# The short branch's output product as seven half-block products in two duals, later modulations moved, gates through half-width buffers

## The chip, the cores and the metric

The kernel runs on one core of a Trainium2 chip. The metric is the device time of one execution in microseconds (us); a figure for a kernel is the median of its runs. A profile is one further execution, recorded by the hardware profiler. Engines are named as the profile names them: PE (TensorE: matrix products), DVE (VectorE), ACT (ScalarE), POOL (GpSimd), SP (SyncE, here only a queue that issues transfers).

## The reference, cut to what matters

One layer of a streaming encoder on x of 1024 tokens by 1024 channels, in fp32:

```
h    = rms_norm(x) * (1 + sc1) + sh1                 # sh, sc, g: "modulations", silu(c) @ w_ada + b_ada
proj = h @ w_in                                      # 7168 columns: b, c, v, u, u's gate, gates a and b
y_a  = (b * dwconv3(c * v)) @ w_short_out            # short branch: its operand is called q below
y_b  = silu(layer_norm(dwconv31(u * sigmoid(gl)))) @ w_conf_out
x    = x + g1 * ((sigmoid(ga) * y_a + sigmoid(gb) * y_b) @ w_o)
x    = x + g2 * ffn(rms_norm(x) * (1 + sc2) + sh2)   # SwiGLU, then a last rms_norm
```

## The kernel before, in words

**Numbers.** Each fp32 operand of a product is split in two (`split` L311, `split_w` L198): a high part, cast to fp32r by ACT (L314 for activations, L205 for weights, called `..h` and `wh`), and a low part, source minus high part (`..l` on DVE, L315; `wl`, L206, on DVE or on POOL). `mm3` then needs three matmuls per product of two 128-blocks and 512 tokens: L283 (wh, high), L284 (wh, low), L286 (wl, high). In the changed kernel these are L288, L289, L291; the splits stand at L206, L207, L319 and L320.

**Stages.** Tokens lie on the free axis in two halves h of 512; a channel block is 128 wide. In order on PE: a lead with the first columns of `w_in` and the block `gb`; twelve **duals** (`win_dual`, L565 on) for the other 48 column blocks; the short branch's product `ya` (L757 to L762); the conformer branch's `yb`; `mix` with `w_o`; the feed-forward part. A dual computes four column blocks for both halves by Strassen-Winograd: seven products of half the depth, named "1" "2" "6" "5" "7" "3" "4" in their order, each 2 banks x 4 depth blocks x 3 = 24 matmuls, 168 where the plain form takes 192. Banks x, y, z are three pairs of PSUM banks; a product's result is carried from one bank to the next by ACT copies ("1" into y; "6" and "5" into small tiles `v`, L626) and joined by DVE (L583, L594). The weight blocks of a dual are loaded by SP, added by POOL (L228, L229, L230, L232) and split with the low part on POOL.

**The short branch before.** The q tiles (128 x 1024, eight of them) are finished in the duals, stored to DRAM by SP (L528), and read again during the last dual, number 11: `q_load` (L552) reads two tiles behind each of its products "1", "2", "6", "5" and splits both halves at once. `ya` then runs eight column blocks, each 8 depth blocks x 2 halves x 3 = 48 matmuls, 384 in all, one weight block of `w_short_out` for each column block. Its results are multiplied by the gate a on DVE (L762); the gates were stored to DRAM by the duals, one 128 x 1024 tile at a time (L642, on ACT's queue), and come back by POOL's queue (L760).

**Beside it.** The convolution of 31 taps runs on DVE through all duals (L671, its accumulator in PSUM). Its result u is summed over the blocks on POOL into `tot` (L691, two adds for each block), and `ln_mean` (L698) turns these sums into the mean with two small products `mu`; `ln_square` (L711 to L719) reads u back from DRAM (`cv`) and sums the squares; `ln_rstd` makes `var`. In the kernel before, `mu` follows the first column block of `ya`. The second 24 of the 48 modulations (L264 on DVE: a row product of a loaded 512 KB block with `cs`, sum on the fly) are in `ya` (six behind column blocks, two at the end) and in `yb` (16).

**Order.** Every engine works its own list in order; the lists come from the order of the code through a scheduler. Tiles are taken from rotating pools: `uc` (128 x 1024 tiles: u, q, cv, sc), `g` (128 x 512 tiles: gates, v, sq), `hl` (split halves). A tile can be filled only when the last reader of what lay there before is done, so a load can wait for an engine.

Of the kernel before, what the change touches and what calls it, by code (L numbers as in the profile page):

```python
# [39 lines left out]
P = 128  # L40
# [43 lines left out]
CONV_DUALS = 11.2  # L84
AT_READS = {"7": 4.5, "3": 5.5, "4": 6.5}
# [22 lines left out]
def block_kernel(ctx: ExitStack, tc: tile.TileContext, x0, xT, c, vecs, ada, w_first, w_plain, w_duals,  # L108
# [102 lines left out]
    def dual_units(mats, n, early=False, eng=nc.vector):  # L211
# [7 lines left out]
        def unit(m):  # L219
            if early:  # L220
                get(*{"1": ("11",), "2": ("12",), "6": ("21", "22", "11"), "3": ("12",), "4": ("22",)}.get(m, ()))
            elif m == "1":
                get("11", "12", "21", "22")
            if m in "12":
                return split_w(a["1" + m], n, (), eng)
# [7 lines left out]
            return split_w(a[{"6": "11", "5": "s1", "7": "21", "3": "12", "4": "22"}[m]], n, (), eng)  # L233
# [9 lines left out]
    plan += [(w_short[k], 1024, (), nc.gpsimd) for k in range(KC)]  # L243
# [307 lines left out]
    qT = [[None, None] for _ in range(KC)]  # L551

    def q_load(j):

        t = uc_tile("q", T)
        nc.sync.dma_start(t, q_dram[j])
        for h in range(2):
            qT[j][h] = split(t[:, halves[h]], hl_tile, f"q{j}{h}")

    def win_dual(d, pairs, x, y, z):  # L560
# [4 lines left out]
        def c11(p, e, kind, j, *more):  # L565
# [6 lines left out]
            elif kind == "p":  # L572
                e["t"] = uc_tile(f"p{j}", T + SK - 1)
                nc.vector.memset(e["t"][:, : SK - 1], 0.0)
                e["b"] = [e["t"][:, SK - 1 + h * H : SK - 1 + (h + 1) * H] for h in range(2)]
            else:
                e["t"] = [uc_tile("sig", T) for _ in range(2)]
                e["b"], e["c"] = ([t[:, s] for s in halves] for t in e["t"])
            nc.scalar.activation(e["b"][0], y[p], AF.Sigmoid if kind == "g" else AF.Copy)

        def c22(p, e, kind, j, *more):
# [4 lines left out]
            if kind == "p":  # L586
                e["z"] = src
            else:
                e["z"] = e["c"][1] if kind == "g" else src
                nc.scalar.activation(e["z"], src, AF.Sigmoid, scale=-1.0)  # L590
            return add

        def c12(p, e, kind, j, *more):
# [7 lines left out]
            nc.scalar.activation(e["b"][1], z[p], AF.Sigmoid)  # L601
            return add

        def c21(p, e, kind, j, *more):
# [7 lines left out]
            nc.scalar.activation(e["c"][0], x[p], AF.Sigmoid, scale=-1.0)  # L612

        banks = {"1": x, "6": x, "7": x, "4": x, "2": y, "5": z, "3": z}
        for m in PRODUCTS:
# [15 lines left out]
            if d == len(PAIRS) // 2 - 1 and m in "1265":  # L631
                for j in range(2):
                    q_load(2 * "1265".index(m) + j)
        for e, (kind, j, *more) in zip(st, pairs):
            if kind == "p":
                short_conv(j, e["t"], x)
            elif kind == "q":
                for i in range(2):
                    q_store(j + i)
            elif kind == "g":  # L640
                for g, t in zip((j, *more), e["t"]):
                    nc.scalar.dma_start(gate_dram[g], t)  # L642
# [55 lines left out]
    def ln_mean():  # L698
        mu = []
        for h in range(2):  # L700
            mps = ps_tile("mu")
# [19 lines left out]
    def ln_rstd(sqs):  # L721
        rs = []
        for h in range(2):
            var = ps_tile("var")
# [11 lines left out]
    def act_b(k, h):  # L736
        z = cv[k][:, halves[h]]
        with ExitStack() as order:
            if (KC - 1, 1) in ma:
# [5 lines left out]
    def next_b(k, h):  # L745
# [3 lines left out]
        modulation(24 + KC * h + k)  # L749
# [7 lines left out]
    for j in range(KC):  # L757
        for h, ps in enumerate(col_block(next_w(), qT, (0, 1), "ya")):
            ga = g_tile("ga")
            nc.gpsimd.dma_start(ga, gate_dram["a", j][:, halves[h]])  # L760
            ma[j, h] = s_tile(f"ma{j}{h}")
            ma["ins"] = nc.vector.tensor_tensor(ma[j, h], ps, ga, ALU.mult).ins  # L762
        if j == 0:
# [6 lines left out]
        if j == KC - 2:  # L770
            act_b(0, 0)
        if j < KC - 2:
            modulation(16 + j)


    modulation(22)
    modulation(23)
# [426 lines left out]
```

## Time and profile before

| | us |
|---|---|
| median of 3 runs | 1505.06 |
| lowest and highest run | 1504.25 to 1505.3 |
| span of the profiled execution | 1501.2 |
| time of the profiled execution | 1502.96 |
| of the span: PE busy | 1469.3 |
| DVE busy | 1141.0 |
| ACT busy | 623.1 |
| POOL busy | 538.2 |

The profiled execution took 1.76 us more than its span and lies 2.1 us under the median. Starts in the trace are us from the start of the span. A row of the timeline gives start, duration, engine, line, operation, output<-input and how many instructions are drawn together, then in brackets how long the engine was idle before and what released it. A row of the windows gives for a stretch its length and each engine's busy time with the instructions in brackets, the granted clock of TensorE as a share, the busy share of the DMA engines and GB/s. A row of the waits gives who waited for whom: total, times, longest.

### The profile page before, as it was taken

How to read it: one execution, taken by the hardware profiler on the slowest of the kernel's cores; microseconds unless marked ns; L12 is line 12 of the kernel's file. 1: busy time of each engine (PE TensorE's matmuls, PEld its weight loads, DVE VectorE, ACT ScalarE, POOL GpSimd, SP SyncE). 2: the span in 40 equal slices, each digit the busy share in tenths (PEclk: the TensorE clock that was granted, in tenths of full speed). 3: DMA queues.
4: the chain of work that ended last, by engine and by line, in shares of the span. 5: the costliest groups of instructions: out<-in, count | busy, mean ns of one | idle time of the engine just before them, and what ended most of it. 6: DMA issues, size and time to landing. Idle time of an engine off the chain costs nothing.

```text
span 1501.2 us, 17711 instructions
## 1 busy us (share of the span) xinstructions
PE 1469.3 (98%) x6455; PEld 1202.0 (80%) x6455; DVE 1141.0 (76%) x1569; ACT 623.1 (42%) x896; POOL 538.2 (36%) x467
## 2 busy tenths in 40 slices
PE   6999999999999999999999989999999999999997
PEld 2788888888888788887788868888888888888887
DVE  7994999887887984777767789776666665667755
ACT  4653433443343353244345454444444443222235
POOL 0037777777767773410121001111000016444005
PEclk9999999999999999999999989999999999999999
DMA  9522223232222268555765337544444449998403
GB/s 352 207 64 74 94 71 112 70 108 75 98 71 85 99 261 299 167 175 175 231 207 183 126 98 236 200 169 153 152 149 150 153 148 351 364 324 256 141 28 112
DMA packets 82697, 247.24 MB, mean 165 GB/s; under 512 B 9521, under 2 KB 11697, under 8 KB 82610
## 3 DMA queue, kind: packets, MB, share of 16 engines
q1 hardware_dynamic: 41776, 137.91, 27.4%
q0 software_dynamic: 36944, 95.44, 19.2%
q10 hardware_dynamic: 3890, 12.78, 2.2%
q8 instruction: 50, 0.82, 0.2%
q14 instruction: 37, 0.30, 0.1%
HBM read 183.69 MB, written 62.39 MB: 164 GB/s over the span
## 4 chain that ended last, share of the span: by engine, by line
PE 93%; DVE 4%; issue 1%; ACT 1%; DMA 1%; POOL 0%; POOLq 0%; ACTq 0%; DVEq 0%
PE x L286 11%; PE x L284 11%; PE x L283 10%; PE z L283 7%; PE z L284 7%; PE z L286 7%; PE y L284 6%; PE y L283 6%; PE y L286 6%; PE ya L284 2%; PE mix L286 2%; PE mix L284 2%; PE ya L283 2%; PE ya L286 2%; PE mix L283 2%; PE yb L283 2%
## 5 line engine op out<-in xcount | busy, mean ns | idle before, releaser
L205 ACT CAST wh<-raw 128x1024 fp32r<-128x1024 f32 (+2 forms) x257 | 259.4, 1010 | 482.8 <-PE z L284 122.0
L206 POOL TENSOR_TENSOR wl<-raw,wh 128x1024 fp32r<-128x1024 f32 x92 | 227.2, 2471 | 131.1 <-ACT wh L205 130.9
L206 DVE TENSOR_TENSOR wl<-raw,wh 128x1024 fp32r<-128x1024 f32 (+2 forms) x165 | 188.4, 1142 | 52.7 <-ACT wh L205 50.0
L671 DVE SCALAR_TENSOR_TENSOR c<-diff,vec,c 128x512 f32<-128x512 f32 x248 | 178.6, 751 | 3.3
L930 POOL DMA_DIRECT2D hid<-stage x71 | 37.9, 534 | 358.7 <-DVE stage L323 353.0
L283 PE MATMUL x<-th,wh 128*128 128x512 f32 x240 | 93.4, 389 | 0.0
L284 PE MATMUL x<-tl,wh 128*128 128x512 f32 x240 | 93.4, 389 | 0.0
L286 PE MATMUL x<-th,wl 128*128 128x512 f32 x240 | 93.4, 389 | 0.0
L671 DVE SCALAR_TENSOR_TENSOR c<-u,wsum,c 128x512 f32<-128x512 f32 x112 | 84.1, 751 | 1.8
L264 DVE CUSTOM_DVE_ANT_0 raw<-raw,cs,vec 128x1024 f32<-128x1024 f32 x24 | 35.5, 1486 | 50.6 <-DMA raw<-in_ada 50.6
L283 PE MATMUL z<-th,wh 128*128 128x512 f32 x168 | 65.4, 389 | 0.0
L284 PE MATMUL z<-tl,wh 128*128 128x512 f32 x168 | 65.4, 389 | 0.0
L286 PE MATMUL z<-th,wl 128*128 128x512 f32 x168 | 65.4, 389 | 0.0
L228 POOL TENSOR_TENSOR raw<-raw 128x1024 f32<-128x1024 f32 x12 | 29.8, 2482 | 95.0 <-DVE wl L206 94.2
L322 ACT CAST stage<-g 128x512 fp32r<-128x512 f32 x62 | 38.3, 621 | 52.0 <-DMA hid<-stage 25.1
L323 DVE TENSOR_TENSOR stage<-g,stage 128x512 fp32r<-128x512 f32 x62 | 42.5, 688 | 20.5 <-ACT stage L322 20.4
L956 POOL DMA_DIRECT2D th<-hid x71 | 38.1, 537 | 52.0 <-PE x L286 28.3
L283 PE MATMUL yb<-zsh,wh 128*128 128x512 f32 x128 | 50.0, 391 | 2.8 <-DVE gb L793 2.8
L283 PE MATMUL x<-t2h,wh 128*128 128x512 f32 x120 | 47.7, 400 | 5.1 <-ACT wh L205 2.8
L286 PEld LDWEIGHTS x<-th,wl 128*128 128x128 f32 x240 | 45.1, 188 | 9.4
L283 PEld LDWEIGHTS x<-th,wh 128*128 128x128 f32 x240 | 45.1, 188 | 9.3
L284 PEld LDWEIGHTS x<-tl,wh 128*128 128x128 f32 x240 | 45.1, 188 | 9.3
(1012 smaller groups left out, 4263.8 us busy)
## 6 DMA issues: line engine op xcount, KB each, us to landing
hid<-stage POOLq DMA_DIRECT2D x71, 512.0 KB, 4.0
raw<-in_w_fi SPq DMA_DIRECT2D x50, 512.0 KB, 4.3
raw<-in_w_duals SPq DMA_DIRECT2D x48, 512.0 KB, 3.5
th<-hid POOLq DMA_DIRECT2D x71, 256.0 KB, 5.9
tl<-hid POOLq DMA_DIRECT2D x71, 256.0 KB, 6.0
ada<-in_ada SPq DMA_DIRECT2D x24, 512.0 KB, 5.8
raw<-in_ada SPq DMA_DIRECT2D x24, 512.0 KB, 4.5
raw<-in_w_fo SPq DMA_DIRECT2D x24, 384.0 KB, 6.2
```

What stands on the lines that cost most here:

```text
L205: nc.scalar.copy(wh, raw)
L206: lo = lo_engine.tensor_tensor(wl, raw, f32(wh), ALU.subtract)
L228: eng.tensor_tensor(a["s1"], a["21"], a["22"], ALU.add)
L264: nc.vector.tensor_tensor_reduce(out=raw, in0=raw, in1=cs, scale=1.0, scalar=col(V_ADA, b), op0=ALU.mult, op1=ALU.add, accum_out=modc(b),)
L283: nc.tensor.matmul(ps, wh, xh, start=first, stop=False, skip_group_check=again)
L284: nc.tensor.matmul(ps, wh, xl, start=False, stop=False, skip_group_check=again)
L286: mm3.ins = nc.tensor.matmul(ps, wl, xh, start=False, stop=last, skip_group_check=again).ins
L322: nc.scalar.copy(hi, src)
L323: nc.vector.tensor_tensor(lo, src, f32(hi), ALU.subtract)
L671: tap.ins = nc.vector.scalar_tensor_tensor(out=out, in0=src[:, s : s + H], scalar=wt, in1=acc, op0=ALU.mult, op1=ALU.add).ins
L930: nc.gpsimd.dma_start(hid_dram[key], s)
L956: nc.gpsimd.dma_start(t, hid_dram[key][:, s])
```

## The change

**The product.** `ya` becomes two duals of seven products, in this order of (dual, product): (0,"1") (0,"2") (1,"1") (1,"2"), then "6" "5" "7" "3" "4" of dual 0, then of dual 1. That makes 14 x 24 = 336 matmuls. The weights are cut in half blocks, four for each dual; POOL adds them (eight adds), and splits the low parts of "1" and "2", while DVE splits those of the other five. Half of the q blocks stay in their tiles (`sc[4]` to `sc[7]`), the other four are stored and read again, all four behind product "1" of dual 11. `q_operands` forms and splits the operands product by product (28 splits in place of 16, and 16 sums or differences on DVE). The results are carried from bank to bank as in the other duals.

**Where things stand.** `mu` now comes behind the third product in the code. Nine of the 24 later modulations move into duals 0 to 8 (behind their product "2"), eight into the first half of `yb`, seven into the first half of `mix`. Gates leave the duals as 28 half tiles of 128 x 512 in place of 14 whole tiles, each with a store of its own on ACT's queue; the gates a are read back by SP in place of POOL.

```diff
+MOD_DUALS = 9
...
-    plan += [(w_short[k], 1024, (), nc.gpsimd) for k in range(KC)]
+    ya_order = [(d, m) for d in range(2) for m in "12"] + [(d, m) for d in range(2) for m in PRODUCTS[2:]]
+    ya_units = [dual_units([w_short[d, m] for m in range(4)], 1024, True, nc.gpsimd, {m: nc.vector for m in "65734"})
+                for d in range(2)]
+    plan += [ya_units[d][m] for d, m in ya_order]
...
+    def gate_out(g, h, src, t, scale=1.0):
+
+        nc.scalar.activation(t, src, AF.Sigmoid, scale=scale)
+        nc.scalar.dma_start(gate_dram[g][:, halves[h]], t)
...
     def q_load(j):
 
-        t = uc_tile("q", T)
-        nc.sync.dma_start(t, q_dram[j])
-        for h in range(2):
-            qT[j][h] = split(t[:, halves[h]], hl_tile, f"q{j}{h}")
+        sc[j] = uc_tile("q", T)
+        nc.sync.dma_start(sc[j], q_dram[j])
+
+    tq = {m: [None] * KH for m in PRODUCTS}
+
+    def q_block(k, i):
+        return sc[k + KH * (i // 2)][:, halves[i % 2]]
+
+    def q_operands(m):
+
+        for k in range(KH):
+            b11, b12, b21, b22 = (q_block(k, i) for i in range(4))
+            if m == "6":
+                nc.vector.tensor_tensor(b11, b11, b12, ALU.subtract)
+                t2 = g_tile("t2")
+                minus(t2, b11, b22)
+                tq[m][k] = split(t2, hl_tile, "tq")
+                minus(b21, t2, b21)
+                continue
+            if m == "7":
+                nc.vector.tensor_tensor(b12, b22, b12, ALU.subtract)
+            tq[m][k] = split({"1": b11, "2": b21, "5": b11, "7": b12, "3": b22, "4": b21}[m], hl_tile, "tq")
...
-            if d == len(PAIRS) // 2 - 1 and m in "1265":
-                for j in range(2):
-                    q_load(2 * "1265".index(m) + j)
+            if m == "2" and d < MOD_DUALS:
+                modulation(16 + d, uc_tile("ada", D))
+            if d == len(PAIRS) // 2 - 1:
+                if m == "1":
+                    for j in range(KH):
+                        q_load(j)
+                if m != "4":
+                    q_operands(m)
...
-    for j in range(KC):
-        for h, ps in enumerate(col_block(next_w(), qT, (0, 1), "ya")):
-            ga = g_tile("ga")
-            nc.gpsimd.dma_start(ga, gate_dram["a", j][:, halves[h]])
-            ma[j, h] = s_tile(f"ma{j}{h}")
-            ma["ins"] = nc.vector.tensor_tensor(ma[j, h], ps, ga, ALU.mult).ins
...
+    r0, r1, r2 = banks
+    ya_banks = [{"x": r0, "y": r1, "z": r1}, {"x": r2, "y": r1, "z": r0}]
...
+        for p in range(2):
+            ps = bank[p]
+            for k in range(KH):
+                c0 = (p * KH + k) * P
+                mm3([ps], slice(c0, c0 + P), w, [tq[m][k]], m in "15" and k == 0, k == KH - 1, m not in "15")
+            if m == "1":
+                nc.scalar.copy(ya_banks[d]["y"][p], ps)
+            elif m in "65":
+                ya_rest[p, m] = s_tile("v")
+                nc.scalar.copy(ya_rest[p, m], ps)
...
+    for i, (d, m) in enumerate(ya_order):
+        ya_product(d, m)
+        if i == 2:
             mu = ln_mean()
-        if j < 5:
-            for i in range((0, 1, 3, 5, 7)[j], (1, 3, 5, 7, 8)[j]):
-                ln_square(i)
-        if j == 5:
+        elif i == 3:
+            q_operands("4")
+        elif 4 <= i < 8:
+            for j in range(2 * i - 8, 2 * i - 6):
+                ln_square(j)
+        elif i == 9:
             rl = ln_rstd(sqs)
...
+            if h == 0 and j < KC - 1:
+                modulation(16 + MOD_DUALS + KC + j)
```

The scheduler puts the first product of the new `ya` ahead of the last two products of dual 11. Three places show it; brackets name the engines or transfers that an instruction waits for.

PE's list in the kernel before, around the end of product "7" of dual 11 (bank z, `th`); `h41h` is product "3":

```order
L283 MATMUL z_984<-th_946,wh_3749 128x512
L284 MATMUL z_984<-tl_947,wh_3749 128x512
L286 MATMUL z_984<-th_946,wl_3750 128x512
L283 MATMUL y_981<-h41h_673,wh_3802 128x512 [waits Activation_49]
L284 MATMUL y_981<-h41l_674,wh_3802 128x512
L286 MATMUL y_981<-h41h_673,wl_3803 128x512 [waits Pool_49]
```

The same place in the changed kernel; `tqh` and `tql` are the halves of the operand of (0,"1"):

```order
L288 MATMUL z_984<-th_946,wh_3778 128x512
L289 MATMUL z_984<-tl_947,wh_3778 128x512
L291 MATMUL z_984<-th_946,wl_3779 128x512
L729 MATMUL mu_4596<-tot0_975,ones_97 128x512 [waits Pool_49]
L729 MATMUL mu_4599<-tot1_976,ones_97 128x512 [waits Pool_49]
L288 MATMUL x_979<-tqh_3712,wh_3947 128x512 [waits Activation_49]
L289 MATMUL x_979<-tql_3713,wh_3947 128x512 [waits DVE_49]
L291 MATMUL x_979<-tqh_3712,wl_3948 128x512 [waits Pool_49]
```

The two `mu` and the 24 matmuls of (0,"1") moved in ahead of product "3", which then opens with `y_981<-h41h_673` as before and still waits for ACT there: for the copy of product "5" out of bank y.

ACT's list in the kernel before, up to that copy's second half (`v_3832`) and the weights of the first column block of `ya` (`wh_3888`):

```order
L205 CAST wh_3854<-raw_3571 128x1024 [waits PE_49,Pool_49]
L626 COPY v_3832<-y_982 128x512 [waits PE_49]
L314 CAST q60h_3836<-q_3834 128x512 [waits DMAHW6_49]
L314 CAST q61h_3840<-q_3834 128x512
L314 CAST q70h_3846<-q_3844 128x512 [waits DMAHW7_49]
L314 CAST q71h_3850<-q_3844 128x512
L590 ACTIVATE sig_3712<-v_3818 128x512 [waits DVE_49,Activation_49]
L205 CAST wh_3888<-raw_3886 128x1024 [waits PE_49,Pool_49]
```

The changed kernel's, from the weights of (0,"1") (`wh_3947`) to the copies of product "5" (`v_3859`, `v_3873`); `q_3710` is the fourth q tile read again, `wh_3999` the weights of (0,"2"):

```order
L206 CAST wh_3947<-raw_3945 128x1024 [waits DMAHW6_49,PE_49,Pool_49]
L730 ACTIVATE tot0_975<-mu_4596 128x512 [waits PE_49]
L319 CAST tqh_3724<-q_3710 128x512 [waits DMAHW7_49]
L730 ACTIVATE tot1_976<-mu_4599 128x512 [waits PE_49]
L319 CAST tqh_3762<-sc4_2697 128x512
L319 CAST tqh_3766<-sc5_2942 128x512
L319 CAST tqh_3770<-sc6_3419 128x512
L319 CAST tqh_3774<-sc7_3426 128x512
L319 CAST tqh_3813<-t2_3811 128x512 [waits DVE_49]
L206 CAST wh_3999<-raw_3997 128x1024 [waits DMAHW4_49,PE_49,Pool_49]
L319 CAST tqh_3821<-t2_3819 128x512 [waits DVE_49]
L651 COPY v_3859<-y_981 128x512 [waits DVE_49]
```

The copies now stand behind the casts of the new operands and behind `wh_3999`, and the first of them waits for DVE, where it waited for PE alone: its tile is one that DVE's `tql_3814` still reads (`t2_3811`).

DVE's list in the kernel before, from the sixth q tile to the two sums of products "5" and "7" (`v_3818`, `v_3832`):

```order
L315 TENSOR_TENSOR q51l_3798<-q_3791,q51h_3797 128x512 [waits PE_49,Activation_49]
L315 TENSOR_TENSOR q60l_3837<-q_3834,q60h_3836 128x512 [waits DMAHW6_49,PE_49,Activation_49]
L315 TENSOR_TENSOR q61l_3841<-q_3834,q61h_3840 128x512 [waits PE_49,Activation_49]
L583 TENSOR_TENSOR v_3818<-z_983,v_3818 128x512 [waits PE_49]
L315 TENSOR_TENSOR q70l_3847<-q_3844,q70h_3846 128x512 [waits DMAHW7_49,Activation_49]
L315 TENSOR_TENSOR q71l_3851<-q_3844,q71h_3850 128x512 [waits Activation_49]
L583 TENSOR_TENSOR v_3832<-z_984,v_3832 128x512 [waits PE_49]
```

The changed kernel's eleven instructions from the low part of the fourth operand block (`tql_3725`) to `tql_3814`:

```order
L320 TENSOR_TENSOR tql_3725<-q_3710,tqh_3724 128x512 [waits DMAHW7_49,PE_49,Activation_49]
L576 TENSOR_TENSOR q_3710<-q_3710 128x512 [waits DMAHW3_49,DVE_49,Pool_49]
L320 TENSOR_TENSOR tql_3763<-sc4_2697,tqh_3762 128x512 [waits PE_49,Activation_49]
L332 SCALAR_TENSOR_TENSOR t2_3835<-q_3710,sc7_3426 128x512 [waits DMAHW2_49,DVE_49]
L320 TENSOR_TENSOR tql_3767<-sc5_2942,tqh_3766 128x512 [waits PE_49,Activation_49]
L332 SCALAR_TENSOR_TENSOR sc4_2697<-t2_3811,sc4_2697 128x512 [waits DVE_49]
L320 TENSOR_TENSOR tql_3771<-sc6_3419,tqh_3770 128x512 [waits PE_49,Activation_49]
L332 SCALAR_TENSOR_TENSOR sc5_2942<-t2_3819,sc5_2942 128x512 [waits DVE_49]
L320 TENSOR_TENSOR tql_3775<-sc7_3426,tqh_3774 128x512 [waits PE_49,Activation_49]
L332 SCALAR_TENSOR_TENSOR sc6_3419<-t2_3827,sc6_3419 128x512 [waits DVE_49]
L320 TENSOR_TENSOR tql_3814<-t2_3811,tqh_3813 128x512 [waits PE_49,Activation_49]
```

All eleven have both their inputs in SBUF tiles, and the first of them waits for the load of `q_3710`. That load waits on SP's queue for POOL's second `tot` add of the last convolution block (`tot1` += `u7`), whose tile it fills. POOL's own list there runs: `wl` of dual 11's product "4", the two `tot` adds, `wl_3948`, an add of half blocks (L230), `wl_4000` of (0,"2"), two more adds, and `wl_4492` of (1,"1").

More of the change, by code (lines that the diff above doesn't have):

```diff
@@ L585, in c22 @@
                 return minus_times(sc[j + 1][:, halves[1]], src, sc[j + 1][:, halves[1]])
[L586 to L590, printed above, removed]
+            e["z"] = src
+            if kind == "g":
+                gate_out(more[0], 1, src, src, -1.0)
+            elif kind == "u":
+                nc.scalar.activation(src, src, AF.Sigmoid, scale=-1.0)
             return add
```

61 lines of the change are left out of this document (37 added, 24 removed).

## The prediction

> **What bounds the kernel now.** I read the page first: which engine is busy, and what the chain that ends last is made of.
>
> ```profile
> PE 1469.3 (98%) x6455; PEld 1202.0 (80%) x6455; DVE 1141.0 (76%) x1569; ACT 623.1 (42%) x896; POOL 538.2 (36%) x467
> PE 93%; DVE 4%; issue 1%; ACT 1%; DMA 1%; POOL 0%; POOLq 0%; ACTq 0%; DVEq 0%
> ```
>
> PE is busy for 98% of the span and is 93% of the chain, so a matmul less is time less, as long as PE doesn't have to wait in its place. Then the waits of PE, to see where it waits already.
>
> ```profile
> PE yb L283 <- DVE gb L793: 2.8, 2, 1.6
> PE x L283 <- ACT wh L205: 2.8, 1, 2.8
> PE x L283 <- ACT t2h L322: 2.3, 1, 2.3
> PE x L283 <- ACT x L623: 0.8, 1, 0.8
> ```
>
> They are few; around the short branch's product, between 540 and 660 us, there is none. Last the windows, for the stages that the change touches: a saturated stretch of the duals (147 to 252), the end of dual 11 (to 572.2), and `ya` in two pieces.
>
> ```profile
> 147.00:252.00 105.00, 104.21 (x460) 85.99 (x459) 101.25 (x149) 42.05 (x59) 75.57 (x34) 1.00 0.30 101
> 532.00:572.20 40.20, 40.20 (x179) 33.31 (x178) 30.93 (x35) 23.65 (x38) 25.76 (x13) 1.00 0.80 294
> 572.20:612.00 39.80, 39.80 (x174) 32.26 (x173) 24.06 (x35) 11.84 (x17) 15.06 (x11) 1.00 0.65 243
> 612.00:663.00 51.00, 51.00 (x223) 41.55 (x222) 30.97 (x43) 13.21 (x17) 11.53 (x13) 1.00 0.55 180
> ```
>
> After PE come PEld, DVE, ACT and POOL. In `ya` PE has no gap, with DVE at 60%. The stage pays in full for fewer matmuls, but only while the operands come in time.
>
> **The matmuls removed.** Six matmuls of `ya` go from start to start in 1.36 us:
>
> ```profile
> 561.41 0.39 PE L283 MATMUL y<-h41h,wh 128*128 128x512 f32 x1
> 572.29 0.39 PE L283 MATMUL ya<-q00h,wh 128*128 128x512 f32 x1
> 573.65 0.39 PE L283 MATMUL ya<-q10h,wh 128*128 128x512 f32 x1
> ```
>
> That is 0.227 each. 384 become 336: 48 x 0.227 = **-10.9 us**. One product of 24 takes 5.44. The two `mu` are only moved.
>
> **The first product, (0,"1").** I walk the lists on the axis of the trace before, from 561.4, where product "7" of dual 11 ends and "3" began. PE's next are the two `mu`, then (0,"1"). Four kinds of rows price the walk: ACT's weights, cast and copy; POOL's low part and `tot` add; and the transfers.
>
> ```profile
> 551.15 1.04 ACT L205 CAST wh<-raw 128x1024 fp32r<-128x1024 f32 x1
> 552.10 0.61 ACT L314 CAST q30h<-q 128x512 fp32r<-128x512 f32 x1
> 552.62 0.58 ACT L626 COPY v<-z 128x512 f32<-128x512 f32 x1
> 557.33 2.57 POOL L206 TENSOR_TENSOR wl<-raw,wh 128x1024 fp32r<-128x1024 f32 x1 [1.98 <-ACT wh L205]
> 570.72 2.40 POOL L206 TENSOR_TENSOR wl<-raw,wh 128x1024 fp32r<-128x1024 f32 x1 [1.01 <-ACT wh L205]
> L691 POOL TENSOR_TENSOR tot<-tot,u x16: 1284/1298/1763, 186.3 to 561.6; 128x512 f32<-128x512 f32 x16
> L702 PE MATMUL mu<-tot,ones x4: 591/592/592, 583.2 to 584.5; 128*128 128x512 f32 x4
> DMA to landing us min/median/max: 4.2/6.8/8.7
> raw<-in_w_short SPq DMA_DIRECT2D x8, 512.0 KB, 5.1
> cv<-cv SPq DMA_DIRECT2D x8, 512.0 KB, 5.8
> ```
>
> (The eighth row is of the loads `q<-q`, L556; four `mu` begin within 1.3 us, so they take 1.7.) `wl` on POOL ends at 559.9, the two `tot` adds at 561.2 and 562.4. So `mu` waits next to nothing, and PE is through with it at 563.2. POOL then needs 2.4 for `wl_3948`: 564.9. PE asks for it at its third matmul, 563.7, and waits 1.2. The load of `q_3710` can start at 562.4. With the shortest of the `q<-q` landings, since only one or two other loads are in flight, it lands at 566.6; cast 567.2, low part on DVE 567.9. PE stands at the fourth depth block at 566.5 and waits 0.7 and then 0.5. Together **+2.5**, bounds 1 (everything but the third matmul in time) and 5.1 (a q landing at the median). (0,"1") ends at 571.1.
>
> **Product "3" of dual 11.** It waits for the copy of product "5" out of bank y. What stands before this copy are the eleven DVE instructions of the third place shown. DVE's rate and its trouble are in these rows:
>
> ```profile
> 556.96 0.68 DVE L315 TENSOR_TENSOR q50l<-q,q50h 128x512 fp32r<-128x512 f32 x1
> 557.56 2.89 DVE L315 TENSOR_TENSOR q51l<-q,q51h 128x512 fp32r<-128x512 f32 x1
> 560.38 1.78 DVE L315 TENSOR_TENSOR q60l<-q,q60h 128x512 fp32r<-128x512 f32 x1
> 562.08 1.78 DVE L315 TENSOR_TENSOR q61l<-q,q61h 128x512 fp32r<-128x512 f32 x1
> 559.87 3.44 POOL L691 TENSOR_TENSOR tot<-tot,u 128x512 f32<-128x512 f32 x2
> 600.49 3.69 DVE L713 TENSOR_TENSOR cv<-cv,tot 128x512 f32<-128x512 f32 x6
> 601.42 5.04 POOL L206 TENSOR_TENSOR wl<-raw,wh 128x1024 fp32r<-128x1024 f32 x1
> ```
>
> Six undisturbed DVE instructions take 3.69, 0.61 each; eleven from 567.2 end at 574.0, and the copy at 574.6. PE has waited since 571.1: 3.5 us. Below that there is a floor from ACT alone: `wh_3999` can start only when (0,"1") is all but over (570.9), then 1.04, a cast 0.52 from start to start, and the copy 0.58 make 573.0, a wait of 1.9.
>
> But POOL works there too. A DVE instruction with both inputs in SBUF stands still beside POOL: `q51l`, of the size of the 0.68 us `q50l` before it, lasts 2.89 and ends 0.55 after POOL's `wl`; then DVE and the `tot` adds take turns. POOL's L230 add needs a block whose load starts behind `wl_3948` (564.9), plus 5.1: 570.0 to 572.4. `wl_4000` is ready (`wh_3999` at 571.9) and follows after one DVE instruction, 573.0 to 575.4. Taking turns, both fall among the eleven: 4.8 more, copy over at 579.4, a wait of **8.3**. The row at 601.42 speaks the other way: there POOL stood back for a run of DVE instructions and lost 2.6 us. I take 8.3, because the nearest rows are the q splits, the same kind of instruction as these; bounds 1.9 and 8.3.
>
> The Trainium skill ("SBUF — State Buffer", section "Who interferes with whom") says that a DVE instruction with two SBUF inputs contends with a GpSimd instruction that reads SBUF, and that the order of issue decides who blocks. By that rule POOL would have waited at 601.42 for one instruction and not for four; the trace differs. By the rule the wait would be 8.3, by that row alone 3.5.
>
> **The clock.** A wait of this length lowers the granted clock:
>
> ```profile
> 870.83 0.73 PE L283 MATMUL x<-t2h,wh 128*128 128x512 f32 x2 [2.28 <-ACT t2h L322]
> 873.05 0.63 PE L286 MATMUL x<-t2h,wl 128*128 128x512 f32 x1
> 873.48 0.63 PE L283 MATMUL z<-t1h,wh 128*128 128x512 f32 x1
> 874.00:876.00 2.00, 2.00 (x7) 1.58 (x6) 2.00 (x4) 2.00 (x4) 0.00 (x0) 0.53 0.00 0
> ```
>
> After a wait of 2.28 us, matmuls come every 0.43 instead of 0.23, with 0.53 of the clock; that lasts some nine matmuls, 9 x 0.2 = **+1.8**, bounds 0 and 2.4.
>
> **The copies of (1,"1").** (1,"2") adds to a bank that ACT fills from (1,"1"), after DVE has read (0,"2") out of it. Ahead of that read on DVE stand the operands of "5", "7" and "3", and the means taken off the first `cv` tiles, whose loads start only behind those operands. Walked on from 579.4: POOL's next three (L231, L232, `wl_4492`) each hold DVE once between 580 and 592; the operands that free the first `cv` load are done at 593.5, plus 5.8 makes 599.3, and 13 instructions of 0.61 with a copy end at 607.8. PE, with two products, 21 matmuls, a product and 6 matmuls (99 in all, 22.4 us) and the slow clock, asks for it at 603.6. **+4.2**; without POOL in the way the same walk ends at 597.5 for a demand at 597.3, so 0.2; bounds 0 and 8.4 (POOL's L234 and `wl_4524` as well). A second fall of the clock, up to 1.8, I take at nothing: it gives DVE the time that the next products wait for.
>
> **Duals.** Nine modulations, 1.49 each, enter DVE's list, three of them in the window 147 to 252 where DVE has 101.25 of 105:
>
> ```profile
> L264 DVE CUSTOM_DVE_ANT_0 raw<-raw,cs,vec 128x1024 f32<-128x1024 f32 x24 | 35.5, 1486 | 50.6 <-DMA raw<-in_ada 50.6
> ```
>
> There 3 x 1.49 = 4.5 go into 3.75 free. Convolution taps can slip into later duals, whose DVE has more room, so most is hidden: **+0.7**, bounds 0 and 4.5. The same row shows DVE idle for 50.6 us before modulations whose block had not landed; the new places keep that risk, within this bound. The 14 more gate stores on ACT's queue lie on an engine that is 42% busy.
>
> **yb and mix.** Eight modulations leave `yb`, 11.9 us of DVE. Its 2.8 us of waits for `gb` come from gate tiles that DVE frees late: **-2.0**, bounds -2.8 and 0. Seven go to `mix`, where PE waits for nothing; up to +2 if a block lands late and holds DVE, taken at nothing. The eight POOL adds are in the walk above or beside it.
>
> **The sum.** -10.9 + 2.5 + 8.3 + 1.8 + 4.2 + 0.7 - 2.0 = +4.6. The profiled execution took 1502.96, so **1507.6**. The median of the runs before is 2.1 above that execution; I leave the number on the execution's own scale and let the range cover the 2.1.
>
> **The rivals.** *POOL stands back* (as at 601.42): the wait for product "3" is 3.5 and the copies of (1,"1") are in time: -10.9 + 2.5 + 3.5 + 1.8 + 0 + 0.7 - 2.0 = -4.4, 1498.6, faster. It is decided by whether the eleventh DVE instruction ends by 575. For it speaks that DVE has the eleven in a row; against it, that each low part waits for ACT and the q splits did too, and lost. *Half of each*: one POOL instruction gets in (a wait of 5.9) and the later copies wait 2: 1502.9, no difference. *DVE and POOL as one resource in the whole stage*: from 567 to `yb` I count in DVE's list 116 instructions, ten of them low parts of weights and three modulations, some 79 us, and 12 POOL instructions of 2.4, 29 us. If none overlap, `yb` starts near 675.7 instead of the 668.5 of my sum, +7.2: 1514.8. Against it: 24 of these DVE instructions read PSUM, and the window 147 to 252, with DVE's taps reading PSUM, holds 101 us of DVE and 76 of POOL in 105.
>
> **How the numbers follow.** My forecast 0.40, POOL standing back 0.28, half 0.20, one resource 0.12. The range 1496 to 1517 leaves out about 2 in 10: below, the first rival with the bounds of `yb`, duals and clock (-2.6); above, my sum with the second fall of the clock, 4.2 more at the copies, `yb` at 0, and part of the last rival. A measurement of this kernel tells about 0.2%, 3 us, from no change. Faster by more: the first rival and a little of the half, 0.30. Within: most of the half and the low edge of my forecast, 0.23. Slower: 0.47.
>
> **What would show it.** In the profile of the changed kernel: 48 matmuls less; PE's waits with a row of product "3" for ACT of 8 us (3.5 by the first rival), one for POOL's `wl` of about 1.2, and one for the copies into bank y; the eleven DVE rows with two of about 3 us among them; a granted clock near 0.5 for 4 us after 579; `yb`'s wait for `gb` shrunk. I am wrong if the load of `q_3710` starts much earlier than 562, if DVE's eleven end by 575, or if the waits of PE moved into the duals.

## The result, and the profile after

| us | before | changed |
|---|---|---|
| median | 1505.13 (5 runs, 1504.25 to 1505.64) | 1510.31 (5 runs, 1508.69 to 1513.26) |
| profiled execution | 1502.96 | 1510.87 |

The ratio is 1.0035 (95% interval 1.0022 to 1.0049): 5.2 us slower, 0.35%. The forecast was +4.6. The two profiled executions differ by more, 7.9, because the one before lies 2.2 under its median and the one after 0.6 over its own. Below, profiles are compared with profiles and medians with medians.

The page of the changed kernel, PE's row and the chain that ended last:

```profile
PE 1464.3 (97%) x6407; PEld 1195.4 (79%) x6407; DVE 1188.7 (79%) x1615; ACT 642.2 (43%) x926; POOL 545.7 (36%) x455
PE 74%; issue 12%; DVE 6%; POOL 3%; DMA 2%; ACT 1%; POOLq 0%; ACTq 0%; DVEq 0%; SPq 0%
```

The 48 matmuls are gone (6455 to 6407). PE's busy time fell by only 5.0 us, mostly since matmuls at a low clock count as busy for longer. PE's share of the chain fell from 93% to 74%. Of these 19 points 11 went to "issue" (1% to 12%), time in which the engine waited for nothing that the profile shows; DVE rose from 4% to 6% and POOL from 0% to 3%. So the page says only that PE no longer runs through. The waits of PE between 330 and 760 us say where:

```profile
PE y L288 <- ACT v L651: 7.6, 1, 7.6
PE x L288 <- ACT wh L206: 3.5, 1, 3.5
PE z L288 <- ACT z L648: 1.4, 2, 0.8
PE x L288 <- DVE v L813: 1.3, 1, 1.3
PE x L291 <- POOL wl L207: 1.2, 1, 1.2
PE x L288 <- ACT x L648: 1.1, 1, 1.1
PE y L288 <- ACT y L805: 0.5, 1, 0.5
```

The rows of L648 lie in earlier duals. The other five lie where the short branch's new product is made: 7.58 + 3.51 + 1.26 + 1.20 + 0.45 = 14.0 us, where there was no wait before. The waits of `yb` for `gb` are gone. The timeline gives their places (start, duration, engine, line; in brackets the wait ahead), and the starts of `mu`, `yb` and `mix`:

```profile
562.25 1.88 PE L729 MATMUL mu<-tot,ones 128*128 128x512 f32 x4
565.80 0.50 PE L291 MATMUL x<-tqh,wl 128*128 128x512 f32 x1 [1.20 <-POOL wl L207]
578.71 0.79 PE L288 MATMUL y<-h41h,wh 128*128 128x512 f32 x1 [7.58 <-ACT v L651]
584.85 0.43 PE L291 MATMUL y<-h41h,wl 128*128 128x512 f32 x1
607.17 0.50 PE L288 MATMUL x<-tqh,wh 128*128 128x512 f32 x1 [3.51 <-ACT wh L206]
608.59 0.62 PE L288 MATMUL y<-tqh,wh 128*128 128x512 f32 x1 [0.45 <-ACT y L805]
641.01 0.50 PE L288 MATMUL x<-tqh,wh 128*128 128x512 f32 x1 [1.26 <-DVE v L813]
672.87 0.39 PE L288 MATMUL yb<-zsh,wh 128*128 128x512 f32 x1
759.91 0.39 PE L288 MATMUL mix<-mg00h,wh 128*128 128x512 f32 x1
```

From the end of product "7" of dual 11 (562.25, where `mu` begins) to the first matmul of `yb` (672.87) I call it **the stage** from here on: 110.6 us. In the kernel before it runs from 561.41 to 662.85, 101.4; with 10.9 us of matmuls less it would be 90.5. So 20.1 us were lost in it: 14.0 of waits, and the rest mostly slow matmuls behind them (4.7, worked out below). `yb` shrank from 90.5 (662.85 to 753.32) to 87.0.

What made the wait of 7.58 stands in the timelines of DVE, ACT and POOL:

```profile
566.79 0.69 DVE L320 TENSOR_TENSOR tql<-q,tqh 128x512 fp32r<-128x512 f32 x1 [15.22 <-ACT tqh L319]
568.79 0.69 DVE L332 SCALAR_TENSOR_TENSOR t<-q,sc 128x512 f32<-128x512 f32 x1
569.39 2.89 DVE L320 TENSOR_TENSOR tql<-sc,tqh 128x512 fp32r<-128x512 f32 x1
572.20 2.83 DVE L332 SCALAR_TENSOR_TENSOR sc<-t,sc 128x512 f32<-128x512 f32 x1
574.95 0.68 DVE L320 TENSOR_TENSOR tql<-sc,tqh 128x512 fp32r<-128x512 f32 x1
...
569.35 2.38 POOL L230 TENSOR_TENSOR raw<-raw 128x1024 f32<-128x1024 f32 x1 [3.60 <-DMA raw<-in_w_short]
572.11 2.38 POOL L207 TENSOR_TENSOR wl<-raw,wh 128x1024 fp32r<-128x1024 f32 x1 [0.37 <-ACT wh L206]
...
578.07 0.59 ACT L651 COPY v<-y 128x512 f32<-128x512 f32 x1 [5.53 <-DVE tql L320]
```

DVE stood idle for 15.22 us before the low part of the fourth q tile. Two of its instructions then lasted 2.89 and 2.83, each over the time of one POOL instruction, where the rows around them last 0.69. The copy that product "3" waits for had to come behind them. The queue of SP shows why the fourth q tile was late, and how the lateness went on:

```profile
562.86 0.33 SPq L564 DMA_DIRECT2D q<-q  x1
592.72 2.13 SPq L738 DMA_DIRECT2D cv<-cv  x4
```

The load of the fourth q tile (`q_3710`) was issued at 562.86, right after POOL's two `tot` adds (560.31 plus 2.52), the last readers of the buffer. The first loads of `cv` were issued at 592.72, behind the operands. The chain of waits runs straight through them, in this order of time:

```profile
592.72 6.08 DMA cv<-cv
598.90 1.33 DVE cv L740
...
606.73 0.46 DVE sq L746
607.25 0.69 DVE ma L554
607.97 0.58 ACT y L805
608.59 0.62 PE y L288
```

The windows show the clock at the two long waits (columns as before: length, then busy time of PE, PEld, DVE, ACT and POOL, the granted clock, DMA share, GB/s):

```profile
571.20:574.60 3.40, 0.00 (x0) 0.00 (x0) 3.40 (x2) 1.35 (x2) 2.91 (x2) 1.00 0.00 0
574.70:584.90 10.20, 6.19 (x15) 4.84 (x16) 10.20 (x12) 3.41 (x7) 5.25 (x2) 0.50 0.22 78
585.00:588.00 3.00, 3.00 (x15) 2.46 (x14) 2.83 (x6) 2.45 (x4) 0.00 (x0) 1.00 0.23 91
608.90:612.20 3.30, 3.30 (x9) 2.54 (x8) 3.30 (x5) 3.30 (x7) 0.00 (x0) 0.50 0.66 181
```

The clock fell 3.5 us into the first wait, and was low for 10.2 us, beyond the wait's end. From 578.71 to 585.12 there are 15 matmuls in 6.41 us where 3.4 were due: 3.0 lost. From 608.59 to 612.34 nine took 3.75 in place of 2.04: 1.7 lost.

### The profile page after: what moved, and what is told of

Same layout as the page of the kernel before. It is cut to its first block, busy times and chain, and to the rows that moved or that the text cites. A ratio compares the mean times of both kernels' runs of the same rounds, so it can differ in the third digit from the quotient of the medians.

```text
span 1509.1 us, 17719 instructions
## 1 busy us (share of the span) xinstructions
PE 1464.3 (97%) x6407; PEld 1195.4 (79%) x6407; DVE 1188.7 (79%) x1615; ACT 642.2 (43%) x926; POOL 545.7 (36%) x455
## 4 chain that ended last, share of the span: by engine, by line
PE 74%; issue 12%; DVE 6%; POOL 3%; DMA 2%; ACT 1%; POOLq 0%; ACTq 0%; DVEq 0%; SPq 0%
PE x L288 9%; PE x L291 9%; PE x L289 9%; PE z L288 6%; PE z L289 6%; PE z L291 6%; PE y L288 5%; PE y L289 5%; PE y L291 5%; PE yb L288 2%; PE yb L289 2%; PE yb L291 2%; DVE c L698 1%; PE lead L288 1%; PE lead L289 1%
## 5 line engine op out<-in xcount | busy, mean ns | idle before, releaser
L206 ACT CAST wh<-raw 128x1024 fp32r<-128x1024 f32 (+2 forms) x263 | 265.7, 1010 | 444.1 <-PE x L289 132.8
L207 POOL TENSOR_TENSOR wl<-raw,wh 128x1024 fp32r<-128x1024 f32 x88 | 217.3, 2471 | 117.0 <-ACT wh L206 113.5
L207 DVE TENSOR_TENSOR wl<-raw,wh 128x1024 fp32r<-128x1024 f32 (+2 forms) x175 | 202.3, 1158 | 62.2 <-ACT wh L206 60.3
L230 POOL TENSOR_TENSOR raw<-raw 128x1024 f32<-128x1024 f32 x14 | 38.0, 2717 | 123.9 <-DVE wl L207 93.9
L327 ACT CAST stage<-g 128x512 fp32r<-128x512 f32 x62 | 38.3, 621 | 61.1 <-DMA hid<-stage 29.1
L269 DVE CUSTOM_DVE_ANT_0 ada<-ada,cs,vec 128x1024 f32<-128x1024 f32 x33 | 47.9, 1466 | 16.2 <-DMA ada<-in_ada 16.2
L288 PE MATMUL y<-th,wh 128*128 128x512 f32 x132 | 51.3, 389 | 0.0
```

The source lines that it names most:

```text
L206: nc.scalar.copy(wh, raw)
L207: lo = lo_engine.tensor_tensor(wl, raw, f32(wh), ALU.subtract)
L230: eng.tensor_tensor(a["s1"], a["21"], a["22"], ALU.add)
L269: nc.vector.tensor_tensor_reduce(out=raw, in0=raw, in1=cs, scale=1.0, scalar=col(V_ADA, b), op0=ALU.mult, op1=ALU.add, accum_out=modc(b),)
L288: nc.tensor.matmul(ps, wh, xh, start=first, stop=False, skip_group_check=again)
L327: nc.scalar.copy(hi, src)
```

## The experiments

Two theories stood against each other. **Theory A** is the forecast's own sum: each wait has its own cause and price, so a wait that is taken away gives its time back. **Theory B** is the forecast's last rival: DVE and POOL cannot do their work in the time that the stage gives them, so a wait that is taken away turns up at another place. The stage is read from one profile of each kernel; where it starts differs as well (561.0 to 565.4 us), so its gain and that of the median need not agree. Each time is a median beside the kernel before on the same chip. Every edit is made to the changed kernel except in *mods_only*, which edits the kernel before.

| kernel | median, us | ratio to before (95%) | against before, us | stage, us |
|---|---|---|---|---|
| change | 1510.31 | 1.0035 (1.0022 to 1.0049) | +5.2 | 110.6 |
| own_v | 1515.33 | 1.0072 (1.006 to 1.0084) | +10.3 | 113.1 |
| own_t2 | 1510.0 | 1.004 (1.0025 to 1.0055) | +4.9 | 108.1 |
| pool_later | 1509.16 | 1.0031 (1.002 to 1.0042) | +4.1 | 107.7 |
| mods_only | 1500.01 | 0.9969 (0.9958 to 0.998) | -5.1 | 101.4 |
| early_q | 1504.57 | 1.0 (0.9991 to 1.0008) | -0.3 | 102.7 |
| no_adds | 1503.48 | 0.9992 (0.9983 to 1.0001) | -1.4 | 102.9 |
| dve_adds | 1502.03 | 0.9982 (0.9973 to 0.9991) | -2.9 | 99.4 |
| product_only | 1518.71 | 1.0095 (1.0082 to 1.0109) | +13.8 | 110.4 |
| early_q_dve | 1496.94 | 0.9942 (0.9928 to 0.9956) | -8.6 | 94.3 |

**own_v** gives the copy of product "5" a buffer that doesn't wait for DVE's eleven instructions:

```diff
-                    e[m] = g_tile("v")
+                    e[m] = s_tile("v") if m == "5" and d == len(PAIRS) // 2 - 1 else g_tile("v")
```

> The changed kernel with one edit: in dual 11 the copy of product "5" goes to a tile of the operand pool and not to a small tile that DVE's tql_3814 still reads. PE's order up to product "3" stays. Theory A (the wait before product "3" is the late q tile, DVE's eleven instructions and the shared tile): the copy waits for ACT alone, (0,"1") over at 571, then 1.0 for the weights, three casts of 0.52 and 0.6 for the copy, so PE waits 3.0 +- 0.5 where it waited 7.6, and the kernel is 3 to 5 us faster than the changed one. Theory B (DVE and POOL are full in the whole stage, and the wait only shows where PE happens to meet it): the wait there shrinks as well, but the wait for the copies of (1,"1") grows by as much, and the time stays within 1 us of the changed kernel's.

The waits of PE:

```profile
PE y L288 <- ACT y L805: 4.3, 2, 2.3
PE z L288 <- ACT sig L558: 4.0, 1, 4.0
PE y L288 <- ACT v L651: 3.0, 1, 3.0
PE z L288 <- DVE v L608: 1.9, 1, 1.9
```

The wait for product "3" fell from 7.6 to 3.0, and yet the kernel became 5 us slower: waits of 1.9, 4.0 and twice about 2 came behind it. The stage's waits sum to 15.6, against 14.0. Theory A (3 to 5 us faster than the change) fails here. Theory B has the waits moving, but had put the time within 1 us of the change's; that it became longer by 5 neither had forecast.

**own_t2** takes the other side of the same rotation: the operand of product "6" gets another buffer, so that the gate pool turns faster.

```diff
-                t2 = g_tile("t2")
+                t2 = s_tile("t2")
```

> The changed kernel with one edit: the four t2 tiles of q_operands come from the operand pool, so that the copies of product "5" find small tiles free. The scheduler then leaves PE's order at "7", "3", "4" of dual 11, then (0,"1"), and mu behind the third product. Theory A: no wait over 1 us at product "3" and no fall of the clock there; DVE has the 10.9 us of products "3" and "4" more for its list; the 7.6 us, some 3 us of clock and the 1.2 us for POOL go: 1498 to 1501, faster than before by 0.25 to 0.45%. Theory B: the same DVE and POOL work must still be done between 566 and yb, so new waits of 5 us or more appear in the short branch, and the time stays at 1506 or more.

```profile
PE y L288 <- ACT y L805: 11.1, 3, 8.1
```

The scheduler now puts "3" and "4" of dual 11 ahead of (0,"1") on PE, and there is no wait for "3" at all. In its place stands one of 8.08 at the copies of (1,"1"), and the time is the same as the change's. Theory B again. The load of the fourth q tile is as late as before here (issued at 565.40), so this order of PE alone does not help.

**pool_later** holds POOL's L230 add and the `wl` of (0,"2") until the copy of "5" is done, by a POOL add of 128x1 that reads this copy.

```diff
+                    if d == len(PAIRS) // 2 - 1 and m == "5" and p == 0:
+                        one = e[m][:, :1]
+                        held.append(nc.gpsimd.tensor_tensor(aff2[:, :1], one, one, ALU.add).ins)
```

> The changed kernel with POOL's L230 add and the low part of (0,"2") held behind the copy of product "5", by a 128x1 POOL addition that reads this copy. Nothing else moves up to there. If DVE's instructions with both inputs in SBUF stand still beside POOL: all eleven DVE rows last 0.7, the copy begins near 573.6, and the wait before product "3" is 3.0 +- 0.4 where it was 7.6; the whole gains less than these 4.6, since POOL's work then falls on the next DVE instructions: 1 to 4 us. If POOL isn't what stretches them: two rows of about 2.8 us remain, and the wait stays at 7 to 8.

DVE's timeline, with the first and the last of the eleven, and two instructions of the same form behind them (L327 is the changed kernel's L320):

```profile
570.05 0.69 DVE L327 TENSOR_TENSOR tql<-q,tqh 128x512 fp32r<-128x512 f32 x1 [15.29 <-ACT tqh L326]
576.26 0.69 DVE L327 TENSOR_TENSOR tql<-t,tqh 128x512 fp32r<-128x512 f32 x1
...
578.84 2.23 DVE L327 TENSOR_TENSOR tql<-t,tqh 128x512 fp32r<-128x512 f32 x1
581.60 2.30 DVE L327 TENSOR_TENSOR tql<-t,tqh 128x512 fp32r<-128x512 f32 x1
```

All eleven last 0.69, and the wait for "3" is 3.3. The forecast had worked out 3.5 for eleven undisturbed instructions. So it is POOL that stretched the two. But the stretching only moved behind them (2.23, 2.30), and other waits came: PE waited 4.6 for an ACT `wh` at 607.74 and 1.5 for a `wl`. The stage gained 2.9 us, but it starts 3.2 later than in the change, and the medians of this kernel and the change can't be told apart.

**mods_only** moves the modulations alone, and leaves the product as it was before:

```diff
+            if m == "2" and d < MOD_DUALS:
+                modulation(16 + d, uc_tile("ada", D))
...
-        modulation(24 + KC * h + k)
+        if h == 0:
+            modulation(16 + MOD_DUALS + k)
```

> The kernel before with only the later modulations moved as in the change (nine into duals, eight into the first half of yb, seven into the first half of mix). If the +1.2 us of the duals and the -3.4 us of yb in the changed kernel are the modulations': 1505.1 + 1.2 - 3.4 = 1502.9, and the waits of yb for gb are gone. If they come from the gates' half tiles and their stores: duals and yb stay as in the kernel before, 1505 +- 0.7.

It is 5.1 us faster than the kernel before, more than either case had (1502.9 and 1505). `yb` takes 87.0 with no wait for `gb`, and the end of "7" of dual 11 comes 0.4 earlier than before, not later. The modulations cost the duals nothing that shows.

**product_only** is the other half, the change with the modulations back behind the products of `ya` and in `yb`:

```diff
+        if i >= 6:
+            modulation(10 + i)
```

> The changed kernel with the later modulations at places like those of before: none in the duals, eight behind the last products of the short branch, sixteen in yb, none in mix. The moved modulations alone were worth -5.1 us (1500.0 against 1505.1). If the two parts add up: 1510.3 + 5.1 = 1515.4, yb takes 90 us again and not 87. If they don't (the modulations in the short branch fall on a DVE that is full there): 1518 or more.

It is 13.8 us slower than before. The stage is as long as the change's (110.4), but `yb` takes 93.5, with 5.1 us of waits for DVE: the modulations and the short branch's last results (`ma`) both fall on it there. The halves add to 13.8 - 5.1 = 8.7, the change has 5.2; so moving the modulations seems to be worth more beside the new product, but the intervals (12.3 to 16.4 us for this kernel, -6.3 to -3.0 for *mods_only*) leave that open. The gates' half tiles are in this half too and were not tried apart; the stage starts 0.2 later than in the kernel before.

**early_q** goes for the cause of DVE's idle 15 us. The fourth q tile is loaded into two half tiles of the operand pool, which are free early:

```diff
+        if j == KH - 1:
+            sc[j] = [s_tile("qh") for _ in range(2)]
+            for h in range(2):
+                nc.sync.dma_start(sc[j][h], q_dram[j][:, halves[h]])
+            return
```

> The changed kernel with the fourth q tile read again into two half tiles of the operand pool, so that its load no longer waits for POOL's last tot add, and can go out behind product "1" of dual 11. PE's order is then "7", "3", "4", (0,"1"), and most of the operands stand ahead of 562. Theory A2 (the loss is DVE's idle time of 15.2 us before 566.8, which the late tile causes and which DVE can't make up beside POOL): that idle time goes, the wait before product "3", its clock, and the waits behind it go with it, about 14 of the 18.7 us that the part from product "7" to yb lost beside its matmuls: 1494 to 1498. Theory B (DVE and POOL too full anyway): new waits of over 8 us between 573 and yb, 1505 or more.

The loads are issued at 540.37 in place of 562.86, and the stage falls by 7.9 us. The time lies between the two theories, close to B: 1504.57, with 7.7 us of waits in the stage. "3" and "4" again come ahead of (0,"1"); in *own_t2*, with this order and the late tile, the stage fell by 2.5 only. What is left are waits for POOL, and 0.3 at a copy:

```profile
PE y L291 <- POOL wl L207: 3.7, 2, 1.9
PE z L291 <- POOL wl L207: 3.7, 1, 3.7
```

POOL's timeline, then DVE's, show the contention from the other side:

```profile
556.99 11.10 POOL L207 TENSOR_TENSOR wl<-raw,wh 128x1024 fp32r<-128x1024 f32 x2 [6.59 <-ACT wh L206]
...
556.95 1.28 DVE L332 SCALAR_TENSOR_TENSOR sc<-t,sc 128x512 f32<-128x512 f32 x2
558.15 0.68 DVE L332 SCALAR_TENSOR_TENSOR t<-q,sc 128x512 f32<-128x512 f32 x1
...
562.97 0.68 DVE L614 TENSOR_TENSOR v<-z,v 128x512 f32<-128x512 f32 x1
563.57 6.76 DVE L320 TENSOR_TENSOR tql<-q,tqh 128x512 fp32r<-128x512 f32 x3
```

In this stretch DVE's instructions keep their pace of 0.6 us, and POOL's two `wl` need 11.10 where two alone take about 4.8 (2.4 each). Then three DVE instructions take 6.76 in place of 1.9. So "POOL stands back" and "POOL gets in" both happen, in one kernel, within 15 us.

**no_adds** (first diff) leaves the eight additions of half blocks out, and **dve_adds** (second) puts these additions and the low parts of "1" and "2", 12 POOL instructions in all, on DVE:

```diff
+                if not lo:
+                    eng.tensor_tensor(a["s1"], a["21"], a["22"], ALU.add)
+                    eng.tensor_tensor(a["21"], a["21"], a["11"], ALU.add)
+                    eng.tensor_tensor(a["11"], a["11"], a["s1"], ALU.add)
-            elif m == "3":
+            elif m == "3" and not lo:
```

```diff
-    ya_units = [dual_units([w_short[d, m] for m in range(4)], 1024, True, nc.gpsimd, {m: nc.vector for m in "65734"})
+    ya_units = [dual_units([w_short[d, m] for m in range(4)], 1024, True)
```

> The changed kernel without the eight additions of half blocks of w_short_out on POOL (the weights of products "6", "5", "7", "3" and "4" of both duals of the short branch are then not the right ones); loads, casts, low parts and the rest stay. If POOL's additions beside DVE cost what my walk says: the L230 add no longer falls among the eleven, the wait before product "3" goes from 7.6 to about 5, and with four fewer POOL instructions up to 600 the whole is 5 to 9 us faster than the changed kernel. If DVE's own list is the bound: 0 to 2 us faster.

> The changed kernel with the additions and all low parts of the short branch's weights on DVE: 12 POOL instructions of 2.4 us, 29 us, become 12 DVE instructions of 1.2, 14.4 us. If standing still beside POOL is the larger cost: DVE's eleven rows are even, and the whole is 2 to 6 us faster than the changed kernel. If DVE's own list is the bound: 5 to 10 us slower.

The stage falls by 7.7 and 11.2 us. In *no_adds* the wait for "3" is 3.3 and not the 5 that was expected with one POOL instruction left among the eleven. That one, the `wl` of (0,"2"), is there, but now it stands back: all eleven rows last 0.68 or 0.69, and POOL is let in behind them.

```profile
572.03 5.07 POOL L207 TENSOR_TENSOR wl<-raw,wh 128x1024 fp32r<-128x1024 f32 x1 [6.30 <-ACT wh L206]
...
574.76 0.69 DVE L609 TENSOR_TENSOR v<-z,v 128x512 f32<-128x512 f32 x1
575.36 2.29 DVE L321 TENSOR_TENSOR tql<-t,tqh 128x512 fp32r<-128x512 f32 x1
```

*dve_adds* gains 8 us on the change, more than the 2 to 6 expected, and its eleven rows are even. In it DVE has 12 instructions more, each 1.22, and nevertheless less to do. Its window over its stage, ahead of that of the change:

```profile
564.00:663.30 99.30, 93.74 (x393) 74.09 (x392) 90.94 (x127) 55.98 (x85) 2.91 (x5) 0.98 0.63 215
```

```profile
562.25:672.87 110.62, 96.62 (x394) 76.47 (x393) 96.29 (x115) 56.04 (x86) 36.80 (x17) 0.94 0.56 191
```

DVE is busy for 90.94 with 127 instructions, and for 96.29 with 115: the difference and the 14.6 that the twelve cost are time in which DVE stood still beside POOL, some 20 us of the stage. (The same forms show it: the 14 `sq<-sq` last 952 ns on average in the change, and 685 here.) Of the waits over 1 us in the stage, the one for "3" (3.4, the forecast's 3.5 once more) and one of 1.6 are left.

**early_q_dve** makes both repairs, the lines of *early_q* and of *dve_adds* together:

```diff
+            sc[j] = [s_tile("qh") for _ in range(2)]
...
+    ya_units = [dual_units([w_short[d, m] for m in range(4)], 1024, True)
```

> Both repairs together: the early fourth q tile of early_q and the short branch's additions and low parts on DVE of dve_adds. early_q's remaining waits, 7.4 us, were all for POOL's low parts, which stood still beside DVE; dve_adds' remaining waits were 3.4 at product "3" (late tile) and 1.6 for weights. If the two causes are the two that matter, both groups go: from 1504.6 of early_q less 7.4 and some clock, 1494 to 1498, and DVE gains the 15 us that it stood idle. If DVE's list is too long once it also has POOL's part (94 us of work for some 85): DVE's own low parts come late instead, 5 us or more of waits for DVE's wl, and 1500 or more.

Its window over the stage:

```profile
563.00:657.30 94.30, 92.43 (x393) 74.66 (x392) 84.21 (x110) 49.85 (x75) 10.97 (x8) 0.98 0.65 223
```

The stage is 94.3, 3.8 above the 90.5 that fewer matmuls alone would give. One wait over 1 us stands in it, 1.87 for a `wl` at 565.51. Behind it the clock is 0.50 from 565.9 to 569.3, and nine matmuls take 3.64 in place of 2.04: together 3.5 of the 3.8. At 1496.94 (1495.05 to 1499.4) this kernel beats the one before by 8.6 us and the change by 13.8 (each against the runs on its chip). It also lies 3.5 under *mods_only*: of these kernels with the new product, only the one with both repairs lies below the one that has the moved modulations alone. Of the 20.1 us that the stage lost, the early tile alone returns 7.9, POOL's work on DVE alone 11.2, both together 16.3. So these two are the cause of most of the loss, and they overlap a little. (Up to the start of `yb`, with what lies ahead of the stage, it is 7.3, 9.5 and 15.5.)

## Why the prediction was right, and where it was not

| step | forecast | profile |
|---|---|---|
| 48 matmuls | -10.9 | -10.9 |
| first product (0,"1") | +2.5 | +1.2 |
| wait before product "3" | +8.3 | +7.6 |
| clock behind it | +1.8 | +3.0 |
| copies of (1,"1") | +4.2 | +4.0 (3.51 and 0.45) |
| clock behind them | 0 | +1.7 |
| `v` of the second dual (641.01) | not in the sum | +1.3 |
| rest of the stage | 0 | +1.3 |
| duals | +0.7 | +0.8 |
| `yb` | -2.0 | -3.4 |
| from `mix` to the end | 0 | +1.3 |
| sum | +4.6 | +7.9 (medians: +5.2) |

**The matmuls** went as counted.

**The first product.** POOL's `wl` made PE wait 1.20, as forecast. The late fourth q block didn't. Its load went out at 562.86 (forecast 562.4), and its low parts began at 566.79 (forecast 567.2). But dual 11 ended 0.84 later than in the walk, and `mu` and the first matmuls ran slower than I took them: PE came to this block at 567.5 in place of 566.5, and found it ready. The term was 1.3 too large.

**Product "3".** Right in place, in mechanism and nearly in size. Two of the eleven DVE rows are stretched (2.89 and 2.83), beside just the two POOL instructions that were named. *pool_later* and *dve_adds* show the cause: without POOL there the rows last 0.69 and the wait is 3.3 and 3.4, the lower value that the forecast gave. But that POOL would be let in at once, which the forecast took from the nearest rows, was a choice and in part luck: in *no_adds* POOL's `wl` stood back at these same rows. What decides between the two no run shows.

**The clock** was mis-sized. The forecast took nine slow matmuls from a wait of 2.28 us. There the low clock lasts 3.4 us (872.5 to 875.9 in the kernel before); at the wait of 7.58 it lasted 10.2, and 15 matmuls were slow. The second fall, put at nothing, cost 1.7. Together 2.9 more than forecast.

**The copies of (1,"1")** came as walked: `cv` loads issued at 592.72 (forecast 593.5), landed at 598.8 (599.3), the copy at 607.97 to 608.55 (607.8). The profile's row names `wh` as what ended the 3.51, since ACT's list has the squares of `cv` ahead of that cast; both stand behind the same DVE instructions.

**Duals and `yb`.** +0.8 beside +0.7, but not for the reason given: with the modulations alone moved the duals don't lengthen (-0.4). PE's waits between 60 and 556 us sum to 1.6 before, 1.2 in *mods_only*, 1.7 in *product_only* and 2.5 in the change, so neither half makes the increase alone. What does stays open. It may be no more than the spread: the stage starts at 562.25 in the change, and at 563.99 to 565.43 in *dve_adds*, *own_t2* and *pool_later*, whose edits lie in or behind the last dual. `yb` gained 3.4, more than the 2.8 of its waits for `gb`.

**What was too simple** is the picture of the sum itself. It treats the waits as terms that stand side by side. *own_v* cut the largest of them to 3.0, *own_t2* removed it, and neither gained time, because DVE was late as a whole and the next reader paid. The rival "DVE and POOL as one resource in the whole stage" had a chance of 0.12 and a price of +7.2 on the sum; it describes the experiments better than the forecast does. The changed kernel itself came out between the two: its `yb` starts at 672.87, where the sum had 668.5 and the rival 675.7. (The sum's own terms up to there, from 662.85 and with the duals' +0.7, give 669.5; the rival's price is then 6.2 and not 7.2.) The nearness of +4.6 to the measured +5.2 is in part luck. Errors of both signs lie in the sum (-1.3 and -0.7 at the first two waits, +2.9 at the clock, -1.4 in `yb`), and between the two profiled executions, on whose scale it was made, the difference is 7.9. The other rival, POOL standing back, failed at the eleven rows of the changed kernel, but POOL did stand back elsewhere: in that kernel at 624.26, 5.38 us for one L230 addition, in *no_adds* and in *early_q*.

From `mix` to the end +1.3 is left without a cause; the runs of one kernel spread by 4.6 us.

## What to carry to other kernels

A matmul that is taken away pays only where the engines that make its operands have time left; add up their work in that stage with POOL's beside it, since DVE and POOL together were the bound here and not PE. A wait is worth removing only at its source: two edits that took the largest wait away moved it, and two that let DVE start earlier and kept POOL out of its way left, together, one wait of 1.87. Changes that come as one are worth measuring apart: the modulations alone gained 5.1 us, and the product with the gates' half tiles lost 13.8.

## What the runs showed of the hardware

**Who stands still changes sides.** In the changed kernel POOL's L230 addition and its `wl`, 2.38 us each, stretched two DVE instructions with two SBUF inputs, to 2.89 and 2.83; in *early_q* the same pair of engines gave DVE its full pace for 6 us and POOL 11.10 for two. The Trainium skill ("SBUF — State Buffer", section "Who interferes with whom") has the order of issue decide who blocks, for the length of an instruction. The turns at 569.39 and 572.20 agree; 11.10 us for two do not fit one instruction's length, since more than ten DVE instructions passed meanwhile.

**Where a POOL instruction that stood back was let in.** Its end less 2.4 us tells when it ran: 562.9 in *early_q* (the first of the two ends at 565.27), 574.7 in *no_adds*, 604.1 in the kernel before. Each time DVE had just come to an instruction with one input in PSUM (`v<-z,v` at 562.97 and 574.76, `ma<-ya,ga` at 604.10). At 624.26 in the changed kernel it was let in ahead of a `wl` of DVE, which has both in SBUF, so this is not the only way.

**Moving 128x1024 additions and low parts from POOL to DVE made DVE less busy**: 12 instructions more, 5.4 us less in its stage.

**The length of a wait alone doesn't tell whether the clock falls.** Behind a wait of 1.87 us in *early_q_dve* it fell to 0.50, behind one of 1.86 at the same product in *early_q* it stayed at 1.00, as it did behind 2.99 in *own_v*. Once low, it stayed so for 3.4 us in most places, for 6.8 at the wait of 4.57 in *pool_later*, and for 10.2 at the waits of 7.58 here and 8.08 in *own_t2*. The Trainium skill ("TensorE: Matmul & The Clock Gate", section "Part 1: The HAM clock gate") gives an idle window of about 3.4 us for the fall; the 2.28 us wait of the kernel before, with a clock of 0.53 behind it, is below that, so the measurement differs.
